# A hybrid decoder step on one core: the Down product's seven results in banks of their own, buffers shared with the gated layer, and higher shares of side work

## The chip, the cores and the metric

The kernel runs on one core of a Trainium2 chip. The core's engines run their own instruction queues side by side: TensorE (PE) for matmuls, with its weight loads as PEld, VectorE (DVE), ScalarE (ACT), GpSimd (POOL) and SyncE (SP), which here issues most transfers. The metric is the device time of one execution in microseconds (us); less is better. TensorE's clock has two levels, 1.2 and 2.4 GHz; the profile gives the granted share of the full one, 1.00 or 0.50, or a mean of both over a stretch.

## The reference

One inference step of a decoder layer, for a prompt of 512 tokens and 8 sample requests of 8 tokens (576 columns T in all), everything in f32:

```
u = rms_norm(x, g_mix) @ w_in                  # 2048 -> conv, SSD and attention inputs
y_a = short_conv_mixer(u_a)                    # gated short convolution
y_b = ssd_mixer(u_b, dt_bias, a_log, d_skip)   # state-space scan: log_a = dt * -exp(a_log)
y_c = nsa_mixer(u_c, paged cache)              # compressed, selected and window attention
x = x + concat(rms_norm(y_a), rms_norm(y_b), rms_norm(y_c)) @ w_out
h = rms_norm(x, g_ffn)
x = x + (silu(h @ w_gate) * (h @ w_up)) @ w_down
```

with dt = softplus(dt_raw + dt_bias). New cache rows and states are outputs too.

## The kernel before

**Products.** Each f32 matrix is split into a high part (`split`: ScalarE rounds it to fp32r, names ending in hi) and a low part (VectorE subtracts, names ending in lo), and a product is three matmuls: hi·hi, lo·hi, hi·lo. All matmuls named below have 288 columns (HALF, half of T). A *plain job* computes 128 rows of a product: weight chunks of 128 x 512 are loaded (raw), split (whi, wlo), multiplied into a PSUM tile pg, and evacuated. An in-projection job has 16 blocks of K x 3 x 2 halves = 96 matmuls.

**The order of the work.** The in-projection runs as jobs1, jobs2 and jobs3 (the last two 12 jobs each). `run_group` steps a pump behind each matmul: `pump.run(369.0 * len(job.halves) * ratio)` issues side work up to an estimated cost of that share of the matmul's time; the ratios in `run_jobs` are the shares. The side work is `chain()`: compress, sample attention (page gathers on GpSimd, scores and sums on TensorE with tiles pt and po, softmax on ScalarE and VectorE), prompt attention, and merge_c, which writes the merged heads into S4. `pump.drain(main)` issues what is left of it. Then x, the residual, is loaded in 24 transfers on SyncE (L1708 to L1710), and the jobs of w_out follow with `ssd()` and merge_a as their side work. `ssd()` first loads dtb (dt_bias) and ea (a_log) on SyncE, applies Exp to ea and to a small tile sd on ScalarE, and computes dt and log_a in small VectorE operations on tiles sd0 to sd6; matmuls with triU, tri64 and ones follow.

The order in which each engine takes its instructions comes from a scheduler that follows the order of the code; where buffers of a pool are all in use, the next user waits for the last reader.

**The gated layer** (gate and up) multiplies block matrices by Strassen's seven products instead of eight: for each of the weights' items, seven operands (called "1" to "7", order "1264375") are formed from four quarters by VectorE, split, and multiplied by X. Their hi and lo parts take turns: three of seven come from the buffers `whi`/`wlo`, four from `fhi`/`flo` of a pool fw. An operand is 12 matmuls.

**Down** (w_down) begins with 16 plain jobs (jobs6[0]) whose inputs ghl are loaded from DRAM (go), split into hi and lo. Then come three ranges r of the inner dimension. A range has 8 *items*, each one pair of output blocks mp with seven products (ORDER "1256473", 12 matmuls each, 84 in all), whose results `evac_d` adds to x1T with VectorE, ScalarE and GpSimd; 16 plain jobs of the range stand partly between the items and partly behind them (`rest`), those behind with `range_ops` of the next range as side work, which forms the seven right operands. `w_ops` forms and splits an item's seven weight operands (f0, f1 for hi and lo). The seven results of an item are in PSUM tiles: three in pt, two in the halves of pa, one in po, one in the first half of pb:

```
pa, pb = pg(), pg()
ps = [pt()[:, :HALF] for _ in range(3)] + [pa[:, 0, :HALF], pa[:, 1, :HALF], po()[:, :HALF], pb[:, 0, :HALF]]
for p, n in zip(ps, ORDER):
```

`g_in` computes the activation of a tile of the next range. Results 16 x 128 columns each leave at the end through tiles ots.

Of the kernel before, what the change touches and what calls it, by code (L numbers as in the profile page):

```python
# [33 lines left out]
KC = 4  # L34
# [42 lines left out]
def hybrid_step_kernel(ctx, tc, x_prompt, x_sample, cache_k, cache_v, cache_win_k, cache_win_v,  # L77
# [76 lines left out]
    def close_pool(guard):  # L154
        guard.__exit__(None, None, None)
# [160 lines left out]

    rstdB = consts.tile([128, T], F32, name="rstdB")

    ssq = consts.tile([128, 5], F32, name="ssq")
# [869 lines left out]
    def ssd():  # L1189
        YB = dp.tile([128, 4, T], F32, name="YB")  # L1190
        sq_b = sq_c
        tiny = lambda name, n=8: dp.tile([128, 5, n], F32, name=name)
        dtb = dp.tile([128, 8], F32, name="dtb")
        nc.sync.dma_start(dtb, dram(dt_bias, 0, [[0, 128], [1, 8]]))
        ea = dp.tile([128, 8], F32, name="ea")
        nc.sync.dma_start(ea, dram(a_log, 0, [[0, 128], [1, 8]]))
        dsk = dp.tile([128, 4], F32, name="dsk")
# [489 lines left out]
    run_jobs(jobs1[2:], 0.8)  # L1687
    run_jobs(jobs2, 0.85)
    run_jobs(jobs3, 1.05)
    pump.drain(main)  # L1690
# [189 lines left out]
    def prep(i):  # L1880
# [16 lines left out]
        for n in "1264375":  # L1897
            if g < NE and n in "12":
                continue
            if n == "6":  # L1900
                s2 = ws(s1, a11, OP.subtract)
            if n == "3":
                s4 = ws(a12, s2, OP.subtract)
            src = {"1": a11, "2": a12, "6": s2, "4": a22, "3": s4, "7": s3, "5": s1}[n]
            p = n_op[0] % 7
            n_op[0] += 1
            pool, pre, bufs = (wpool, "w", 3) if p < 3 else (fw, "f", 4)
            hi = pool.tile([128, KC, 128], F32R, name=pre + "hi", tag=pre + "hi", bufs=bufs)
            lo = pool.tile([128, KC, 128], F32R, name=pre + "lo", tag=pre + "lo", bufs=bufs)
            split(hi, lo, src)  # L1910
            out.append((n, hi, lo))
            tick(600)
            yield
# [71 lines left out]

    close_pool(fwg)
    x1g, x1p = open_pool("x1")
# [14 lines left out]
    def out_rows(m):  # L2002
# [3 lines left out]
        ot = evt(512).rearrange("p (a b) -> p a b", a=4)  # L2006
        ots = fp.tile([128, 128], F32, name="ots", tag="ots", bufs=2)
        ps = pt()
# [54 lines left out]
    def load_d(i):  # L2063
# [3 lines left out]
        loaded[i] = []  # L2067
        for h in range(2):
            for q_ in range(2):
                w = fp.tile([128, KC, 128], F32, name="wr", tag="wr", bufs=8)  # L2070
                nc.sync.dma_start(w, dram(w_down, (12 * r + 4 + 4 * h) * 128 * D + mp * 256 + q_ * 128,
# [3 lines left out]
    def w_ops():  # L2075

        for i in range(len(items)):
            a11, a21, a12, a22 = loaded.pop(i)
            s1 = fp.tile([128, KC, 128], F32, name="ws", tag="ws", bufs=2)
            for n in ORDER:  # L2080
# [6 lines left out]
                src = {"1": a11, "2": a12, "3": a12, "4": a22, "5": s1, "6": a11, "7": a21}[n]  # L2087
                hi, lo = [fp.tile([128, KC, 128], F32R, name=f"f{q_}", tag=f"f{q_}", bufs=4) for q_ in range(2)]
                split(hi, lo, src)
# [58 lines left out]
    for r in range(NR):  # L2148
        rest = list(jobs6[1 + r])
        tiles = list(range(plain[1 + r], plain[1 + r] + 4))  # L2150
        for mp in range(KT // 2):
            if r + 1 == NR and mp == 7:
                tiles = list(range(plain[-1], nf))
            i = r * KT // 2 + mp
            u = evt(HALF)
            pa, pb = pg(), pg()
            ps = [pt()[:, :HALF] for _ in range(3)] + [pa[:, 0, :HALF], pa[:, 1, :HALF], po()[:, :HALF], pb[:, 0, :HALF]]
            for p, n in zip(ps, ORDER):
                next(weights, None)
                hi, lo = made.pop((i, n))  # L2160
# [4 lines left out]
                evac_d(mp, n, p, u)  # L2165
                if tiles and (n in "53" or r + 1 == NR):
                    g_in(tiles.pop(0))

            for _ in range((2, 2, 2, 2, 3, 3, 2, 0)[mp] if r + 1 == NR else mp % 2):
                run_group([rest.pop(0)], 0.0)  # L2170
# [10 lines left out]
    close_pool(fg)  # L2181
    close_pool(x1g)
    close_pool(eg)

# [28 lines left out]
```

## Time and profile before

| | before |
|---|---|
| median of 3 runs | 2990.16 us (2987.16 to 2991.98) |
| profiled execution | 2989.67 us, its span 2987.9 us |
| mean granted clock of TensorE | 0.973 |
| TensorE busy | 2837.6 us (95%) |
| VectorE, ScalarE, GpSimd busy | 73%, 43%, 21% |

The span is what the profile covers; the 1.8 us between it and the execution's time lie around it. Times in the trace count from the start of the span. "Busy" is the sum of an engine's instructions without waits. A wait is told as "engine, tile, line <- what ended it".

### The profile page before, as it was taken

How to read it: one execution, taken by the hardware profiler on the slowest of the kernel's cores; microseconds unless marked ns; L12 is line 12 of the kernel's file. 1: busy time of each engine (PE TensorE's matmuls, PEld its weight loads, DVE VectorE, ACT ScalarE, POOL GpSimd, SP SyncE). 2: the span in 40 equal slices, each digit the busy share in tenths (PEclk: the TensorE clock that was granted, in tenths of full speed). 3: DMA queues.
4: the chain of work that ended last, by engine and by line, in shares of the span. 5: the costliest groups of instructions: out<-in, count | busy, mean ns of one | idle time of the engine just before them, and what ended most of it. 6: DMA issues, size and time to landing. Idle time of an engine off the chain costs nothing.

```text
span 2987.9 us, 57523 instructions
## 1 busy us (share of the span) xinstructions
PE 2837.6 (95%) x22006; PEld 2729.2 (91%) x22006; DVE 2170.7 (73%) x4409; ACT 1283.3 (43%) x2432; POOL 641.2 (21%) x672
## 2 busy tenths in 40 slices
PE   7999998787899998999999999999999999999999
PEld 6999997676789887999999999999999999999998
DVE  5566565444586765757899988888888879889874
ACT  5465563222354553335554444444444434444332
POOL 2342342444343320202001101101101102222120
PEclk9999999898999998999999999999999999999999
DMA  7444333554623214357655433333333354333323
GB/s 234 117 130 124 94 90 84 166 161 144 151 60 79 58 50 138 105 159 215 185 182 172 161 101 108 109 106 108 107 109 109 108 180 125 118 103 118 110 70 111
DMA packets 485660, 370.65 MB, mean 124 GB/s; under 512 B 70121, under 2 KB 444880, under 8 KB 485384
## 3 DMA queue, kind: packets, MB, share of 16 engines
q1 hardware_dynamic: 461656, 306.55, 35.2%
q0 software_dynamic: 20944, 55.13, 6.4%
q10 hardware_dynamic: 2784, 5.29, 0.5%
q8 instruction: 174, 2.85, 0.4%
q14 instruction: 102, 0.84, 0.1%
HBM read 312.98 MB, written 51.79 MB: 122 GB/s over the span
## 4 chain that ended last, share of the span: by engine, by line
PE 49%; DVE 5%; DMA 2%; issue 1%; ACT 1%; SPq 0%; POOL 0%; ACTq 0%; DVEq 0%
PE pg L1949 16%; PE pg L434 12%; PE pt L1949 9%; PE po L1949 5%; PE pg L2164 2%; PE pt L2164 2%; DVE f L96 1%; PE pt L434 1%; PE po L2164 1%; DVE wlo L96 1%; DVE x1T L96 1%; DMA raw<-in_w_up_dram 1%; DMA u<-g_d 1%; DVE wr L96 0%; PE pt L128 0%
## 5 line engine op out<-in xcount | busy, mean ns | idle before, releaser
L93 ACT ACTIVATE whi<-raw 128x512 fp32r<-128x512 f32 (+1 forms) x510 | 319.4, 628 | 536.8 <-PE pg L434 260.7
L96 DVE TENSOR_TENSOR wlo<-raw,whi 128x512 fp32r<-128x512 f32 (+1 forms) x510 | 354.1, 696 | 171.3 <-ACT whi L93 143.3
L434 PE MATMUL pg<-hhi,whi 128*128 128x288 f32 (+1 forms) x1440 | 344.6, 319 | 4.8 <-issue 4.0
L1949 PE MATMUL pg<-X,fhi 128*128 128x288 f32 x1656 | 333.6, 297 | 0.5 <-DVE u L96 0.5
L434 PE MATMUL pg<-hlo,whi 128*128 128x288 f32 (+1 forms) x1440 | 326.0, 306 | 8.1 <-issue 4.7
L434 PE MATMUL pg<-hhi,wlo 128*128 128x288 f32 (+1 forms) x1440 | 324.1, 305 | 7.3 <-issue 4.3
L1949 PEld LDWEIGHTS pg<-X,fhi 128*128 128x128 f32 x1656 | 264.8, 188 | 4.5 <-DVE u L96 0.7
L96 POOL TENSOR_TENSOR u<-u 128x576 f32<-128x576 f32 x44 | 70.9, 1616 | 888.3 <-DVE u L96 811.2
L434 PEld LDWEIGHTS pg<-hhi,whi 128*128 128x128 f32 (+1 forms) x1440 | 238.0, 196 | 20.7 <-issue 17.0
L434 PEld LDWEIGHTS pg<-hlo,whi 128*128 128x128 f32 (+1 forms) x1440 | 241.8, 196 | 13.5 <-issue 8.7
L434 PEld LDWEIGHTS pg<-hhi,wlo 128*128 128x128 f32 (+1 forms) x1440 | 241.5, 196 | 9.6 <-issue 5.9
L93 ACT ACTIVATE fhi<-raw 128x512 fp32r<-128x512 f32 x246 | 155.3, 632 | 212.1 <-PE pg L1949 180.9
L1949 PE MATMUL pg<-X,flo 128*128 128x288 f32 x828 | 239.3, 295 | 0.0
L1949 PE MATMUL pt<-X,whi 128*128 128x288 f32 x1168 | 235.8, 295 | 0.0
L434 PE MATMUL pg<-ghl,whi 128*128 128x288 f32 x1280 | 228.8, 298 | 3.9 <-DVE ghl L96 2.6
L96 DVE TENSOR_TENSOR flo<-raw,fhi 128x512 fp32r<-128x512 f32 x246 | 170.2, 693 | 46.3 <-ACT fhi L93 41.9
L434 PE MATMUL pg<-S,whi 128*128 128x288 f32 x1024 | 197.1, 301 | 0.4 <-DVE u L96 0.4
L434 PEld LDWEIGHTS pg<-ghl,whi 128*128 128x128 f32 x1280 | 190.1, 190 | 4.9 <-DVE ghl L96 2.8
L1949 PEld LDWEIGHTS pt<-X,whi 128*128 128x128 f32 x1168 | 188.2, 188 | 0.0
L96 POOL TENSOR_TENSOR x1T<-x1T,u 128x288 f32<-128x288 f32 (+1 forms) x72 | 99.1, 1376 | 392.7 <-ACT u L93 240.5
L1949 PE MATMUL pt<-X,wlo 128*128 128x288 f32 x584 | 172.9, 296 | 0.0
L434 PEld LDWEIGHTS pg<-S,whi 128*128 128x128 f32 x1024 | 159.0, 191 | 1.4 <-issue 0.6
(1343 smaller groups left out, 6979.0 us busy)
## 6 DMA issues: line engine op xcount, KB each, us to landing
wr<-in_w_gate_dram SPq DMA_DIRECT2D x88, 512.0 KB
wr<-in_w_up_dram SPq DMA_DIRECT2D x88, 512.0 KB
raw<-in_w_in_dram SPq DMA_DIRECT2D x144, 256.0 KB
wr<-in_w_down_dram SPq DMA_DIRECT2D x96, 256.0 KB
raw<-in_w_down_dram SPq DMA_DIRECT2D x80, 256.0 KB
raw<-in_w_out_dram SPq DMA_DIRECT2D x64, 256.0 KB
g_d<-u POOLq DMA_DIRECT2D x44, 288.0 KB
u<-g_d SPq DMA_DIRECT2D x40, 288.0 KB
```

The lines of the kernel that those rows point to most:

```text
L93: S.activation(out, in_, func, bias=bias, scale=scale, accum_out=accum)
L96: (eng or V).tensor_tensor(out, a, b, op=op)
L434: PE.matmul(ps[:m, s, :HALF], w[:, k, :m], x[:, s * HALF:(s + 1) * HALF], start=(k0 + k == 0 and n == 0), stop=(k0 + k == n_k - 1 and n == 2))
L1949: PE.matmul(P[n], w[:, k, :], xx, start=(j == 0 and q_ == 0), stop=(j == 7 and q_ == 2))
L2164: PE.matmul(p, w[:, j, :], x, start=(j == 0 and c_ == 0), stop=(j == 3 and c_ == 2))
```

## The change

It has six parts. (1) ea and dtb are loaded at the start, from GpSimd's queue into a pool that lives for the whole kernel, instead of in `ssd()` from SyncE's. (2) The shares of side work rise from 0.85 to 0.95 in jobs2 and from 1.05 to 1.1 in jobs3. (3) The last gated item's first three operands ("1", "2", "6") use the whi/wlo buffers and the other four fhi/flo; before, the count ran on over all items. (4) The pool fw stays open through Down, and Down's w_down loads (in 5 buffers of 128 x 1024) and operand parts use its buffers instead of ones of Down's own (8 of 128 x 512; f0, f1); ots has one buffer instead of two. (5) Result 4 gets the first half of pb, and result 3 a fourth pt tile; pa holds result 6 alone. (6) In the first two ranges a plain job stands behind six of eight items instead of four (six in the items, ten behind them); in the last range the counts of the 16 jobs are dealt out differently, the tiles of g_in come at products 5 and 3 only, and the last ones start at the seventh item.

```diff
+    ea = consts.tile([128, 8], F32, name="ea")
+    dtb = consts.tile([128, 8], F32, name="dtb")
+    nc.gpsimd.dma_start(ea, dram(a_log, 0, [[0, 128], [1, 8]]))
+    nc.gpsimd.dma_start(dtb, dram(dt_bias, 0, [[0, 128], [1, 8]]))
...
-        dtb = dp.tile([128, 8], F32, name="dtb")
-        nc.sync.dma_start(dtb, dram(dt_bias, 0, [[0, 128], [1, 8]]))
-        ea = dp.tile([128, 8], F32, name="ea")
-        nc.sync.dma_start(ea, dram(a_log, 0, [[0, 128], [1, 8]]))
...
-    run_jobs(jobs2, 0.85)
-    run_jobs(jobs3, 1.05)
+    run_jobs(jobs2, 0.95)
+    run_jobs(jobs3, 1.1)
...
-            p = n_op[0] % 7
+
+            p = n_op[0] % 7 if i + 1 < len(items) else len(out)
...
-    close_pool(fwg)
...
-        ots = fp.tile([128, 128], F32, name="ots", tag="ots", bufs=2)
+        ots = fp.tile([128, 128], F32, name="ots", tag="ots", bufs=1)
...
+            w2 = fw.tile([128, KC, 256], F32, name="wr", tag="wr", bufs=5).rearrange("p a b -> p (a b)")
             for q_ in range(2):
-                w = fp.tile([128, KC, 128], F32, name="wr", tag="wr", bufs=8)
+                w = w2[:, q_ * KC * 128:(q_ + 1) * KC * 128].rearrange("p (k c) -> p k c", k=KC)
...
-                hi, lo = [fp.tile([128, KC, 128], F32R, name=f"f{q_}", tag=f"f{q_}", bufs=4) for q_ in range(2)]
+                hi, lo = [fw.tile([128, KC, 128], F32R, name=q_, tag=q_, bufs=4) for q_ in ("fhi", "flo")]
...
-            if r + 1 == NR and mp == 7:
+            if r + 1 == NR and mp == 6:
...
-            ps = [pt()[:, :HALF] for _ in range(3)] + [pa[:, 0, :HALF], pa[:, 1, :HALF], po()[:, :HALF], pb[:, 0, :HALF]]
+            ps = [pt()[:, :HALF] for _ in range(3)] + [pa[:, 0, :HALF], pb[:, 0, :HALF], po()[:, :HALF], None]
             for p, n in zip(ps, ORDER):
+                p = pt()[:, :HALF] if p is None else p
...
-                if tiles and (n in "53" or r + 1 == NR):
+                if tiles and n in "53":
...
-            for _ in range((2, 2, 2, 2, 3, 3, 2, 0)[mp] if r + 1 == NR else mp % 2):
+            for _ in range((0, 2, 3, 4, 4, 3, 0, 0)[mp] if r + 1 == NR else mp % 4 > 0):
...
     close_pool(x1g)
+    close_pool(fwg)
```

**VectorE at the end of jobs3.** Before, from the last operations of merge_c (S4, qT) to the first of the sd chain; wlo belongs to the weights of w_out here, and x1 is the residual:

```order
L96 TENSOR_TENSOR wlo_13503<-raw_13489,whi_13502 128x512
L105 SCALAR_TENSOR_TENSOR S4_13199<-qT_705,cols_193,S4_13199 128x576 x2
L96 TENSOR_TENSOR wlo_13633<-raw_13492,whi_13632 128x512
L100 TENSOR_SCALAR triU_13569<-diff_110 128x128
L100 TENSOR_SCALAR same_13571<-same_13571,fl8_137 64x64
L96 TENSOR_TENSOR tri64_13574<-same_13571,triU_13569 64x64
L96 TENSOR_TENSOR wlo_13707<-raw_13495,whi_13706 128x512
L96 TENSOR_TENSOR x1_13438<-pg_13485,x1_13438 128x288
L96 TENSOR_TENSOR x1_13446<-pg_13485,x1_13446 128x288
L96 TENSOR_TENSOR x1_13439<-pg_13702,x1_13439 128x288
L96 TENSOR_TENSOR sd0_13534<-dtg_165,dtb_13522 128x40
```
Of the change, the same place on VectorE, from the last S4 operation to the first of the sd chain; wlo belongs to the last chunks of jobs3 here:

```order
L105 SCALAR_TENSOR_TENSOR S4_13014<-qT_709,cols_197,S4_13014 128x576 x2
L96 TENSOR_TENSOR u_13302<-pg_13163,rstdB_189 128x576
L96 TENSOR_TENSOR wlo_13308<-raw_13236,whi_13307 128x512
L96 TENSOR_TENSOR wlo_13336<-raw_13272,whi_13335 128x512
L96 TENSOR_TENSOR u_13302<-u_13302,rstdB_189 128x576
L1412 COPY u_13415<-cols2_198 128x8x2
L96 TENSOR_TENSOR sd0_13534<-dtg_165,dtb_191 128x40
L100 TENSOR_SCALAR triU_13569<-diff_110 128x128
L105 SCALAR_TENSOR_TENSOR sd1_13535<-sd0_13534 128x40
L100 TENSOR_SCALAR sd5_13539<-sd0_13534 128x40
L100 TENSOR_SCALAR same_13571<-same_13571,fl8_137 64x64
L96 TENSOR_TENSOR tri64_13574<-same_13571,triU_13569 64x64
```
The S4 operations now end ahead of jobs3's last splits, and the sd chain begins among these, ahead of the evacuations into x1.

**ScalarE between the gated layer and Down.** Before; whi and raw are weights of Down's first plain jobs, ghl the split of their inputs go:

```order
L93 ACTIVATE u_28703<-pt_28590 128x288
L93 ACTIVATE whi_28826<-raw_28816 128x512
L93 ACTIVATE whi_28874<-raw_28818 128x512
L93 ACTIVATE ghl_28790<-go_28782 128x576
L93 ACTIVATE ghl_28793<-go_28783 128x576
L93 ACTIVATE ghl_28796<-go_28784 128x576
L93 ACTIVATE ghl_28799<-go_28785 128x576
L93 ACTIVATE whi_28915<-raw_28820 128x512
```
Of the change; fhi are the first weight operands of Down's items, made from wr and ws:

```order
L93 ACTIVATE u_28703<-pt_28590 128x288
L93 ACTIVATE whi_28825<-raw_28815 128x512
L93 ACTIVATE whi_28873<-raw_28817 128x512
L93 ACTIVATE fhi_29478<-wr_28996 128x512
L93 ACTIVATE fhi_29482<-wr_28999 128x512
L93 ACTIVATE fhi_29495<-ws_29477 128x512
L93 ACTIVATE ghl_28789<-go_28781 128x576
L93 ACTIVATE ghl_28792<-go_28782 128x576
L93 ACTIVATE ghl_28795<-go_28783 128x576
L93 ACTIVATE ghl_28798<-go_28784 128x576
L93 ACTIVATE whi_28914<-raw_28819 128x512
```
Three fhi have moved ahead of the ghl splits, and the whi in front use buffers of other operands of the last gated item.

**TensorE in the first item of Down.** Before, from the end of result 6 (first half of pg_29492) through result 7 (po) into result 4 (second half of the same pg):

```order
L2164 MATMUL pg_29492<-go_29372,f1_29521 128x288
L2164 MATMUL po_29497<-go_28949,f0_29559 128x288 x2
L2164 MATMUL po_29497<-go_28949,f1_29560 128x288
L2164 MATMUL po_29497<-go_29127,f0_29559 128x288 x2
L2164 MATMUL po_29497<-go_29127,f1_29560 128x288
L2164 MATMUL po_29497<-go_29256,f0_29559 128x288 x2
L2164 MATMUL pg_29492<-go_28945,f0_29537 128x288 x2
L2164 MATMUL pg_29492<-go_28945,f1_29538 128x288
```
Of the change, from the end of result 6 through result 4 (pg_29488) to the start of result 7 (po):

```order
L2166 MATMUL pg_29487<-go_29367,flo_29516 128x288
L2166 MATMUL pg_29488<-go_28944,fhi_29532 128x288 x2
L2166 MATMUL pg_29488<-go_28944,flo_29533 128x288
L2166 MATMUL pg_29488<-go_29079,fhi_29532 128x288 x2
L2166 MATMUL pg_29488<-go_29079,flo_29533 128x288
L2166 MATMUL pg_29488<-go_29247,fhi_29532 128x288 x2
L2166 MATMUL pg_29488<-go_29247,flo_29533 128x288
L2166 MATMUL pg_29488<-go_29371,fhi_29532 128x288 x2
L2166 MATMUL pg_29488<-go_29371,flo_29533 128x288
L2166 MATMUL po_29492<-go_28948,fhi_29554 128x288 x2
```
Result 4 has a pg tile of its own and follows result 6 at once; before, it shares result 6's tile and begins when most of result 7 has been issued.

## Rows read from the trace of the kernel before

**Rows 1.** The page: busy time by engine; granted clock of TensorE in 40 slices.

```profile
PE 2837.6 (95%) x22006; PEld 2729.2 (91%) x22006; DVE 2170.7 (73%) x4409; ACT 1283.3 (43%) x2432; POOL 641.2 (21%) x672
...
PEclk9999999898999998999999999999999999999999
```

**Rows 2.** Windows before and in Down: length, busy (instructions) by engine, PEclk, DMA share, GB/s.

```profile
2400.00:2420.00 20.00, 20.00 (x152) 20.00 (x152) 13.22 (x23) 9.21 (x16) 0.00 (x0) 1.00 0.23 66
2580.00:2600.00 20.00, 18.23 (x126) 18.00 (x125) 17.19 (x31) 6.90 (x13) 3.16 (x3) 0.91 0.43 138
```

**Rows 3.** Windows of the seams and of sample attention, same columns.

```profile
1149.90:1190.10 40.20, 27.60 (x155) 25.30 (x153) 22.62 (x71) 6.87 (x17) 5.22 (x6) 0.75 0.70 202
1190.10:1193.60 3.50, 3.50 (x16) 3.44 (x16) 2.06 (x7) 1.05 (x3) 0.00 (x0) 0.50 0.47 149
500.00:800.00 300.00, 236.55 (x2258) 196.21 (x2254) 130.17 (x372) 69.06 (x127) 125.28 (x132) 0.86 0.50 150
2426.17:2436.00 9.83, 6.10 (x26) 5.87 (x27) 6.44 (x7) 2.83 (x5) 4.28 (x4) 0.66 0.88 290
```

**Rows 4.** Waits of TensorE, 2380 to 2990 us: total, times, longest.

```profile
PE pg L2164 <- DVE u L96: 8.4, 9, 1.8
```

**Rows 5.** Waits of TensorE, 1149 to 1194 us.

```profile
PE pt L120 <- DVE sd L105: 6.6, 1, 6.6
PE pg L434 <- DVE wlo L96: 4.9, 1, 4.9
```

**Rows 6.** Timeline of SyncE, 1149 to 1170 us: start, duration, issue.

```profile
1149.85 0.37 SPq L1708 DMA_DIRECT2D x<-xT_d  x1
...
1164.80 0.53 SPq L1710 DMA_DIRECT2D x<-xS_d  x1
...
1166.89 0.37 SPq L1196 DMA_DIRECT2D ea<-in_a_log_dram  x1
```

**Rows 7.** Waits of ScalarE, 1149 to 1194 us.

```profile
ACT ea L93 <- DMA ea<-in_a_log_dram: 6.9, 1, 6.9
```

**Rows 8.** Timeline of VectorE, 1160 to 1180 us: sd, first and last.

```profile
1172.35 0.19 DVE L96 TENSOR_TENSOR sd<-dtg,dtb 128x40 f32<-128x40 f32 x1
...
1178.54 0.42 DVE L1228 COPY lab<-sd 64x512 f32<-64x512 f32 x1
```

**Rows 9.** Waits of TensorE, 490 to 800 us.

```profile
PE po L120 <- issue: 14.8, 27, 1.8
PE po L120 <- ACT pT L93: 13.3, 4, 6.3
...
PE pt L120 <- ACT kT L93: 5.2, 4, 1.8
```

**Rows 10.** Waits of GpSimd, 490 to 800 us.

```profile
POOL vp L271 <- PE po L120: 84.9, 10, 12.7
```

**Rows 11.** Waits of TensorE, 2424 to 2437 us.

```profile
PE pg L434 <- DVE ghl L96: 2.6, 1, 2.6
PE pg L434 <- ACT ghl L93: 1.2, 1, 1.2
```

**Rows 12.** Waits of ScalarE, 2415 to 2437 us.

```profile
ACT whi L93 <- PE po L1949: 8.5, 2, 7.5
```

**Rows 13.** Timeline of TensorE, 2503.5 to 2506 us: idle time and releaser in brackets.

```profile
2505.43 0.79 PE L2164 MATMUL pg<-go,f 128*128 128x288 f32 x4 [1.25 <-DVE u L96]
```

**Rows 14.** Groups of VectorE, 2490 to 2740 us: busy, mean ns, idle before.

```profile
L96 DVE TENSOR_TENSOR f<-wr,f 128x512 fp32r<-128x512 f32 x94 | 66.2, 706 | 1.9 <-ACT f L93 1.4
...
L96 DVE TENSOR_TENSOR f<-ws,f 128x512 fp32r<-128x512 f32 x16 | 28.3, 1768 | 0.0
```

**Rows 15.** Tile rows: durations in ns (least, median, most), first and last start.

```profile
L348 POOL DMA_DIRECT2D rows<-in_norm_ffn_dram x1: 682/682/682, 2.5 to 2.5; - x1
```

**Rows 16.** Tile ots, same columns.

```profile
L2014 DVE COPY ots<-pt x16: 294/295/298, 2926.6 to 2983.2; 64x128 f32<-64x128 f32 x16
L2016 SPq DMA_DIRECT2D out_dram<-ots x16: 467/472/524, 2927.6 to 2983.5; - x16
```

## The prediction

> **What bounds the kernel now.** I read the page's busy times and its row of granted clock first: TensorE works 95% of the span, and the other engines have room [rows 1]. A change that leaves TensorE's instructions as they are (the two programs have 20,733 each) can save only the time in which TensorE stands, or runs at the lower of its two clock levels. So I looked for that time stretch by stretch. At full clock 152 matmuls fill 20.00 us, 0.1316 us each [rows 2]; a stretch's count times 0.1316 is what it needs, and the rest is lost. Four places stand out that the diff touches: the seam between the in-projection and the output projection (155 matmuls in 40.20 us), the 500 to 800 us of sample attention (TensorE busy 236.55 of 300 at 0.86 of the clock), the seam between the gated layer and Down (26 in 9.83) [rows 3], and nine stalls inside Down's items [rows 4]. Everything else of TensorE runs dense and can only be moved.
>
> **A, the first seam (ea and dtb loaded early, shares raised).** The 155 matmuls need 155 × 0.1316 = 20.4 us and take 40.2: 19.8 lost; the next 3.5 us hold 16 at half clock (0.50), 16 × 0.1316 = 2.1, so 1.4 more [rows 3]: 21.2 in all. The chain of waits shows two stops, 4.9 us for a wlo (VectorE, which first finishes the merge of attention's heads, S4) and 6.6 us for sd [rows 5]; half clock behind them is the rest. Behind the second stop stands a queue. pump.drain ends attention; then SP issues 24 loads of x, from 1149.85 to 1165.33, and only then ea, at 1166.89 [rows 6]. ScalarE waits 6.9 us for ea [rows 7], with sd's exponential queued behind it, and VectorE's 25 small sd operations run from 1172.35 to 1178.54 [rows 8] with nothing else to do. TensorE takes its instructions in order, and the matmuls on sd stand ahead of the next projection job.
>
> After: ea and dtb are there from the start, and the higher shares bring the end of attention forward by about a job and a half. The order shows the S4 operations some ten rows ahead of jobs3's last chunks on VectorE, and the sd chain between the last splits of jobs3 and the first of jobs4. Both stops thus have projection work in front of them. I leave one stop of the size of the first, 4.9 less rounding: **−21.2 + 4.2 = −17**. Bounds: −8 (only the ea wait and a part of the half clock behind it go, because the 24 loads of x, which now stand behind five weight loads on SP, hold up the first evacuations) and −21 (all).
>
> **B, what the shares cost.** run_group lets the pump put so much side work behind each matmul; counted in the two orders, sample attention is spread over 8.24 projection jobs' matmuls before and 7.26 after, prompt attention over 11.76 and 11.24. That takes 1.50 jobs × 96 matmuls × 0.1316 = 19 us of cover out of stages in which TensorE already stands 63.45 of 300 us [rows 3]. These matmuls aren't lost, they run later, dense. So the cost is what the stages don't shrink. Of the stops there, 18.5 us wait for ScalarE's pT and kT, a result just asked for; the largest other one, 14.8, waits for nothing the profile shows [rows 9]. GpSimd's page gathers wait 84.9 us for TensorE [rows 10], so most of the chain runs behind TensorE, and less cover makes it run sooner. I let a fifth of the cover return as stops: **+4**. Bounds: 0, and +19 if the stages are as long as their own chains.
>
> **C, the second seam (operands of the last gated item, shared buffers).** 26 matmuls need 3.4 us of the 9.83: 6.4 lost [rows 3]. TensorE waits 2.6 and 1.2 for ghl [rows 11], the split of Down's first inputs; their hi halves stand on ScalarE behind a whi that waited 7.5 us, to the last matmul of the last gated item (po) [rows 12], because that buffer was held by its op "5". Now op "6" of that item holds it, four operations earlier. But the order puts three fhi of w_down ahead of ghl, and the third needs the buffer of op "7", the last but one; an op is 12 matmuls, 1.6 us. The ghl splits thus start about 1.6 us before the item's end instead of after it, and four of them and their lo halves follow. I leave 1.4 us: **−5**. Bounds −1 (the fhi take the place of whi: the wait is for op "7" and the sum of two w_down loads) and −6.4.
>
> **D, Down's items.** VectorE's read of the first half of pa (result 6) and TensorE's writing of the second half (result 4) can't overlap: TensorE stops until that read ends, 9 times, 8.4 us, the longest 1.8 [rows 4]; in one of them it resumes at 2505.43 [rows 13]. All other results have a bank each. The clock stays at 1.00 around the 1.25 us stop, but falls to 0.91 where the longest lies (126 matmuls in 20 us: 16.6 needed, 3.4 lost, 1.8 of it the stop), so 1.6 more [rows 2]. Giving 4 a pg tile and 3 a pt tile removes the cause: 10.0. Against it: two more plain jobs per range leave the run of plain jobs behind the items, so its VectorE work on the next range's operands is divided over 10 jobs instead of 12; a plain job is 24 matmuls, 3.2 us. VectorE is the second busiest, its f<-ws take 1.768 us against 0.706 of f<-wr [rows 14]. I allow 1: **−9**. Bounds −12 (VectorE's backlog in the pairs goes too) and −4 (half of the stops come back as waits for lo splits).
>
> Those long f<-ws run while GpSimd adds to x1T. The Trainium skill ("SBUF — State Buffer", section "Who interferes with whom") states that a VectorE operation with two inputs in SBUF and a GpSimd one exclude each other on a shared read port. By that rule, denser items would meet more such blocks: 16 × 1.06 us in two ranges is what this pattern costs VectorE now, and TensorE only where VectorE is behind. The trace agrees as to the durations.
>
> **E, F, at nothing.** The two early loads cost GpSimd an issue each, like the 0.68 us of the rows load that follows them [rows 15]; ScalarE's first split waits for a weight load until then anyway; 0, at worst +1.4. The single ots buffer: 16 copies from 2926.6 to 2983.2, 3.8 us apart, with an issue of 0.47 us each [rows 16], which leaves 3 us for the store; 0, at worst +1. The last range's table only deals the same 16 plain jobs out differently.
>
> **Sum.** −17 + 4 − 5 − 9 = −27, against the profiled execution: 2989.67 − 27 = 2962.7, **2963 us**. That execution lies 0.5 below the median of 2990.16, so the same sum fits either. All good ends: −21 + 0 − 6.4 − 12 = −39.4, 2950. All bad: −8 + 19 − 1 − 4 + 2.4 = +8.4, 2998. A measurement of this kernel can tell about 0.2%, 6 us, from no change.
>
> **Rivals.**
> Fixed wall (15%): sample and prompt attention keep their length, because each step waits for its own ScalarE and VectorE results; B is +19 and the sum −12: 2978. For it: pT's four stops, up to 6.3 us. Against: the gathers that wait for TensorE.
> VectorE bounds Down (13%): the bank wait goes, but TensorE then waits for lo splits at the next weight load; D is −2 and the sum −20: 2970. For it: VectorE's share in Down; against: items between two plain jobs, in the last range, show no stop but one.
> The seam stays (10%): S4 or the x loads take the place of the sd chain; A is −8, the sum −18: 2972. The bank split not reaching the program is no case, since the order shows 4 and 7 in tiles of their own.
> Slower (7%): with less cover, TensorE's granted clock falls in sample attention. Its stops there already cost 0.14 of the clock [rows 3]. The work is 236.55 × 0.86 = 203 full-speed us; at 0.86 it fills 236.55, at 0.74 it takes 275, 38 more: −27 + 38 = +11, 3001. It decides from a mean clock of 0.75 down (271 us, +34, +7). Against: the clock is full where projection is interleaved, and nine tenths of that stay.
> The Trainium skill ("TensorE: Matmul & The Clock Gate", section "What's actually happening") has the gate follow how busy TensorE has recently been, and thinner cover is what would lower it; the trace agrees in direction, half clock after the two stops of [rows 5], full after 1.25 us ones.
>
> **How the numbers follow.** My forecast has 55% (own range 2955 to 2969); with it the first three rivals make 93%, at 2955 to 2982. The range takes in the good end and a fixed wall with one more small term short: **2950 to 2985**. Slower by over 0.2% is the clock's case and part of a mix of bad ends, 6%; within 0.2% the milder part of both, 9%; faster 85%.
>
> **What would show it.** Right: no wait for ea, and none over 3 us for sd or wlo at the first seam; its window at 25 us instead of 40; no wait of Down's matmuls for u<-pg; under 2 us for ghl. B shows in TensorE's idle time and clock in sample attention, which should be within 5 us of 63. Wrong: a clock there well under 0.86, or new waits of Down's matmuls for f or of its plain jobs for wlo, which would put the gain of D back.

## The result, and the profile after

The changed kernel takes 2962.16 us in the median of 4 runs (2956.48 to 2970.22), the kernel before in the same session 2989.69 (4 runs): a ratio of 0.991, 95% interval 0.9884 to 0.9936. That is 27.5 us less; 2963 was forecast. Run again in another session, it took 2952.8 against 2976.92, 0.9923 (0.991 to 0.9936). The four times spread over 14 us, and the profiled execution is the slowest of them: 2970.22, its span 2968.4, 19.5 below that of before. Sums over its trace are held against those 19.5.

The page of the changed kernel, as in [rows 1]:

```profile
PE 2834.8 (96%) x22006; PEld 2726.6 (92%) x22006; DVE 2169.8 (73%) x4409; ACT 1282.8 (43%) x2432; POOL 643.7 (22%) x674
...
PEclk9999899788999999999999999999999999999999
```
TensorE's matmuls are as many as before and its busy time is nearly what it was; the 19.5 us come out of its idle time, and the dip of its clock around the first seam, in the sixteenth slice, is gone. That of sample attention, the eighth to tenth slice, is still there and reads 7, 8, 8 instead of 8, 9, 8.

Windows of the changed kernel, as in [rows 3]: sample attention, the first 19.98 us behind the last in-projection matmul, and the first 9.83 us behind the gated layer's last:

```profile
500.00:800.00 300.00, 236.39 (x2226) 193.52 (x2224) 128.51 (x367) 68.78 (x126) 131.56 (x135) 0.85 0.48 148
1166.66:1186.64 19.98, 19.98 (x158) 19.23 (x157) 11.99 (x39) 6.39 (x14) 3.64 (x3) 1.00 1.06 289
2426.37:2436.20 9.83, 9.29 (x68) 9.07 (x68) 9.83 (x15) 4.74 (x8) 4.44 (x4) 1.00 0.91 292
```
The first seam holds 158 matmuls in 19.98 us, at full clock and without a gap, where 155 took 40.20 [rows 3]. The second holds 68 instead of 26. In sample attention TensorE stands 63.6 of 300 us, as before, at 0.85 instead of 0.86. But this fixed window now holds 2226 matmuls instead of 2258 [rows 3], so it doesn't show what the stage costs as a whole. The whole of jobs2 and jobs3, before and changed, does:

```profile
477.48:1150.08 672.60, 599.16 (x5265) 526.27 (x5264) 394.13 (x1247) 249.25 (x589) 250.72 (x277) 0.93 0.39 105
```
```profile
482.79:1166.66 683.87, 607.77 (x5265) 533.12 (x5264) 409.87 (x1283) 250.35 (x592) 253.51 (x280) 0.92 0.39 105
```
The same 5265 matmuls take 11.3 us longer. TensorE stands 76.1 us instead of 73.4, which is 2.7 of them; the other 8.6 are busy time, at a lower mean clock.

TensorE's waits from 1149 to 1210 us answer to [rows 5]; all that is left over a microsecond is this:

```profile
PE pg L438 <- DVE wlo L96: 1.3, 1, 1.3
```
From 490 to 800 us they answer to [rows 9]:

```profile
PE po L120 <- issue: 23.7, 40, 1.1
PE pt L120 <- issue: 11.5, 8, 2.8
...
PE po L120 <- ACT pT L93: 0.8, 2, 0.7
```
The long stops for pT have nearly gone, and the ones that wait for nothing shown have grown from 14.8 us in 27 to 23.7 in 40. From 2370 to 2990 us, the whole of Down, they answer to [rows 4] and [rows 11], and these four are all there is:

```profile
PE pt L128 <- issue: 1.0, 1, 1.0
PE pt L2166 <- DVE x1T L96: 0.4, 2, 0.3
PE pg L438 <- DVE u L96: 0.4, 1, 0.4
PE pg L438 <- DVE x1T L96: 0.2, 1, 0.2
```
No stop for u<-pg at result 4 is left of 8.4 us, and none for ghl. ScalarE's timeline at the second seam (start, duration, wait in brackets) shows the order that the prediction was worked from:

```profile
2422.14 0.63 ACT L93 ACTIVATE fhi<-wr 128x512 fp32r<-128x512 f32 x1 [1.77 <-PE pg L1950]
2423.07 0.63 ACT L93 ACTIVATE fhi<-wr 128x512 fp32r<-128x512 f32 x1 [0.30 <-PE pg L1950]
2424.68 0.64 ACT L93 ACTIVATE fhi<-ws 128x512 fp32r<-128x512 f32 x1 [0.97 <-PE pg L1950]
2425.22 0.67 ACT L93 ACTIVATE ghl<-go 128x576 fp32r<-128x576 f32 x1
2426.61 2.17 ACT L93 ACTIVATE ghl<-go 128x576 fp32r<-128x576 f32 x3 [0.73 <-DMA go<-g_d]
```
Three fhi wait for the last gated item's operations, and ghl begins 1.15 us before the gated layer ends at 2426.37; before, it began 0.44 us behind its end, at 2426.61 against 2426.17:

```profile
2426.61 2.39 ACT L93 ACTIVATE ghl<-go 128x576 fp32r<-128x576 f32 x4
```

For the experiments the span is cut at the same instructions in every trace (start of the first projection matmul, end of jobs1 and so on); each cell is one profiled execution. The output projection here runs from the end of jobs3 to its own last matmul; "to items" from the gated layer's end to the first item's first matmul.

| kernel | session | start | jobs1 | jobs2, 3 | output proj. | gated | to items | items |
|---|---|---|---|---|---|---|---|---|
| before | 1 | 15.85 | 461.63 | 672.60 | 280.05 | 953.86 | 58.85 | 436.61 |
| changed | 1 | 18.18 | 464.61 | 683.87 | 259.91 | 955.91 | 52.85 | 423.43 |
| banks alone | 2 | 16.87 | 456.58 | 666.32 | 280.27 | 953.05 | 58.85 | 433.09 |
| table alone | 2 | 16.50 | 457.10 | 666.22 | 280.29 | 954.36 | 58.73 | 432.60 |
| shares alone | 2 | 16.59 | 461.07 | 679.58 | 261.60 | 953.31 | 57.35 | 436.57 |
| early loads alone | 2 | 17.70 | 454.37 | 663.44 | 278.51 | 956.52 | 57.72 | 438.05 |
| changed, again | 3 | 18.03 | 459.12 | 670.04 | 260.82 | 955.28 | 52.70 | 423.31 |
| changed, old item rule | 3 | 17.93 | 456.96 | 682.05 | 260.69 | 956.12 | 56.50 | 422.57 |
| changed, old shares | 3 | 17.41 | 460.70 | 662.11 | 278.54 | 956.04 | 52.98 | 422.82 |
| changed, shares 0.85, 1.15 | 3 | 18.27 | 458.81 | 660.28 | 273.09 | 956.56 | 53.14 | 423.13 |
| changed, own buffers | 4 | 18.12 | 449.33 | 576.64 | 259.99 | 955.27 | 56.55 | 424.40 |
| banks and table | 4 | 16.80 | 446.10 | 573.05 | 280.30 | 954.67 | 58.08 | 423.59 |
| item rule alone | 4 | 16.81 | 445.93 | 569.16 | 277.64 | 953.55 | 57.03 | 437.86 |
| changed, late loads | 4 | 16.58 | 451.07 | 579.71 | 261.58 | 954.08 | 53.49 | 422.95 |

The kernels of a session ran on one chip; sessions 2 to 4 on three different ones. From the output projection on, equal code takes equal time within 1 to 3 us: the output projection takes 277.64 to 280.30 in the five kernels without the higher shares and the early loads, and "to items" 57.35 to 58.85 in the six kernels with the old item rule and the old buffers. jobs1 to jobs3 vary by 5 to 14 us from execution to execution, and jobs2 and jobs3 are another stage altogether in session 4 (below).

### The profile page after: what moved, and what is told of

Its sections match the earlier page's. It is cut to its first block, busy times and chain, and to the rows that moved or that the text cites. A ratio compares the mean times of both kernels' runs of the same rounds, so it can differ in the third digit from the quotient of the medians.

```text
span 2968.4 us, 57509 instructions
## 1 busy us (share of the span) xinstructions
PE 2834.8 (96%) x22006; PEld 2726.6 (92%) x22006; DVE 2169.8 (73%) x4409; ACT 1282.8 (43%) x2432; POOL 643.7 (22%) x674
## 4 chain that ended last, share of the span: by engine, by line
PE 49%; DVE 5%; DMA 2%; issue 1%; ACT 1%; POOL 0%; SPq 0%; ACTq 0%; DVEq 0%; POOLq 0%
PE pg L1950 16%; PE pg L438 10%; PE pt L1950 9%; PE po L1950 5%; PE pt L2166 4%; PE pg L2166 2%; DVE wlo L96 1%; PE po L2166 1%; PE pt L438 1%; DMA raw<-in_w_up_dram 1%; DVE go L96 1%; DVE u L96 1%; DVE x1T L96 1%; DVE flo L96 1%; PE pt L128 0%
## 5 line engine op out<-in xcount | busy, mean ns | idle before, releaser
L93 ACT ACTIVATE fhi<-wr 128x512 fp32r<-128x512 f32 x222 | 140.0, 631 | 219.2 <-PE pg L1950 89.0
L96 DVE TENSOR_TENSOR flo<-wr,fhi 128x512 fp32r<-128x512 f32 x222 | 160.3, 722 | 49.6 <-ACT fhi L93 48.5
```

Of the source, the lines that this page charges most:

```text
L93: S.activation(out, in_, func, bias=bias, scale=scale, accum_out=accum)
L96: (eng or V).tensor_tensor(out, a, b, op=op)
```

## The experiments

**Down: banks alone.** The kernel before with

```diff
-ps = [...3 pt...] + [pa[:, 0, :HALF], pa[:, 1, :HALF], po()[:, :HALF], pb[:, 0, :HALF]]
+ps = [...3 pt...] + [pa[:, 0, :HALF], pb[:, 0, :HALF], po()[:, :HALF], None]    # None: pt()
```

> The kernel before with the bank split of Down's results alone (result 4 in a pg tile of its own, result 3 in a fourth pt tile). Bank theory: the nine stops of 8.4 us in Down's items go, and the lowered clock behind the longest with them: 8 to 11 us faster, about 2980. Rival, VectorE bounds the items: the stops come back as waits for the lo parts of operands, and the gain is 0 to 4 us.

Measured: 2972.01 us against 2979.29, ratio 0.9976 (0.9962 to 0.9989). The 7.3 us lie between the theory's 8 to 11 and the rival's 0 to 4. The stops for u are gone, but the items, all that the edit touches, are only 3.5 us shorter. TensorE's waits in Down of this kernel:

```profile
PE pt L2165 <- DVE x1T L96: 4.9, 4, 2.7
PE pg L434 <- DVE x1T L96: 3.9, 2, 2.0
```
8.8 us in 6 stops for x1T have come in place of 8.4 us in 9 for u. VectorE's timeline ahead of one of them, which ends at 2515.78:

```profile
2499.14 0.68 DVE L96 TENSOR_TENSOR f<-ws,f 128x512 fp32r<-128x512 f32 x1
2499.73 1.92 DVE L96 TENSOR_TENSOR wr<-wr 128x512 f32<-128x512 f32 x1
2501.57 0.44 DVE L96 TENSOR_TENSOR x1T<-pt,x1T 128x288 f32<-128x288 f32 x1
```
VectorE runs from 2496.30 to 2512 us with no gap over 0.1 us, its wr<-wr stretched to 1.92 us, and its reads of finished results (x1T<-pt) come late; TensorE meets the next use of their banks. The VectorE rival holds, with x1T in place of f.

**Down: the table alone.** The kernel before with `mp % 4 > 0` and the last range's new counts and tiles.

> The kernel before with the new table of plain jobs alone (six of eight items followed by one in the first two ranges, the other deal in the last), the results' banks as before. Bank theory: the stops stay where two items follow each other, two pairs a range in the first two instead of four, and the last range has two pairs as well; 2 to 5 us faster. Rival, the plain jobs are what removes the stops, since VectorE catches up behind them: 8 to 11 us faster. If the table costs by VectorE's work divided over fewer jobs, it shows in the run of plain jobs behind the items: up to 4 us slower.

Measured: 2972.8 us, ratio 0.9982 (0.9969 to 0.9996): 6.5 us less, between the two forecasts; items 4.0 us shorter. The waits for u, as in [rows 4]:

```profile
PE pg L2164 <- DVE u L96: 5.0, 6, 1.2
```
Four of the nine stops go, those of the pairs that a plain job now parts, and one comes in the last range, between its first two items, which the new table leaves together. The stops are where the bank theory had them. The run of plain jobs behind the items doesn't get longer by it.

**Down: both.** The kernel before with the two edits above together.

> The kernel before with the bank split and the new table of plain jobs together, nothing else. Alone they shortened the items from 436.6 to 433.1 and 432.6 us, 3.5 and 4.0. Theory (the banks take the stop away, the plain jobs give VectorE the time without which it becomes the next stop): together 422 to 425 us, more than the sum, and 12 to 14 us faster than before, about 0.9955. Rival (they add up, and the shared buffers made the rest of the change's 423.4): 428 to 430 us.

Measured: 2856.3 us against 2872.9, ratio 0.9946 (0.9934 to 0.9958), items 423.59, 13.0 us shorter. The time, 16.6 us less, is beyond the expected 12 to 14, the items are as expected. Alone the edits give 3.5 and 4.0. TensorE's waits in Down over 0.3 us (beside the one at the end):

```profile
PE pg L434 <- DVE ghl L96: 2.6, 1, 2.6
PE pg L434 <- ACT ghl L93: 1.2, 1, 1.2
...
PE pt L2165 <- ACT f L93: 0.7, 1, 0.7
PE pg L2165 <- DVE f L96: 0.5, 1, 0.5
```
Neither u nor x1T is left; the two of ghl belong to the second seam. The theory of the pair holds: the banks remove the stop, and the plain jobs give VectorE the time without which it makes the next one.

**The first seam: shares alone.** The kernel before with 0.95 and 1.1.

> The kernel before with the higher shares of side work alone; ea and dtb are still loaded behind the 24 loads of x. Theory: sample attention costs 4 to 11 us more, and the first stop of the seam (4.9 us for wlo) goes with the half clock behind it, 6 to 10 us; the second (for ea and the sd chain) stays in part. Net -5 to +4 us. Rival, the shares alone bring the whole gain of the seam, 20 us, since the ea load too comes earlier: net -8 to -16.

Measured: 2970.56 us against 2979.29, ratio 0.9972 (0.9959 to 0.9985). Output projection 18.7 us shorter than in the two kernels above it on the same chip (280.3), jobs2 and jobs3 13.3 longer (666.3). The waits of TensorE from 1110 to 1200 us, as in [rows 5]:

```profile
PE pt L120 <- DVE mt L96: 1.5, 1, 1.5
PE pg L434 <- DVE wlo L96: 1.1, 2, 0.6
PE pt L120 <- DVE sq_c L96: 1.0, 1, 1.0
```
Both stops are gone, 6.6 and 4.9 us. The load of ea, still issued in `ssd()`, comes early as well, as the rival had it: SyncE issues it ahead of the 24 loads of x, 12.2 us before jobs3 ends at 1157.24.

```profile
1145.02 0.42 SPq L1196 DMA_DIRECT2D ea<-in_a_log_dram  x1
...
1159.09 0.56 SPq L1708 DMA_DIRECT2D x<-xT_d  x1
```
So the end of attention and the load of ea move together here, and this run doesn't tell which of them counts. The net of 8.7 us lies in the rival's range; the cost of 13.3 is above the theory's 4 to 11. Here too it is mostly busy time: jobs2 and jobs3 of the table alone, and of the shares alone:

```profile
473.60:1139.82 666.22, 597.13 (x5265) 527.66 (x5264) 394.05 (x1247) 248.85 (x589) 250.74 (x277) 0.93 0.38 106
```
```profile
477.66:1157.24 679.58, 607.25 (x5265) 533.88 (x5264) 410.35 (x1284) 250.92 (x594) 250.20 (x280) 0.92 0.38 105
```
TensorE stands 69.1 and 72.3 us in them, so stops are 3.2 of the 13.4 us between these two.

**The first seam: early loads alone.** The kernel before with ea and dtb loaded at the start.

> The kernel before with the early loads of ea and dtb alone. Theory: ScalarE's wait of 6.9 us for ea goes and the second stop of the seam (6.6 us) shrinks to what the sd chain itself takes, with a part of the half clock: 5 to 10 us faster; the start is not later by more than 1.4 us. Rival from the trace of the change, where the first projection matmul stands 2.3 us later and the end of the first 21 jobs 5.3 us later: the two loads delay the start, and the net is only 0 to 5 us.

Measured: 2979.92 us against 2979.29, ratio 0.9999 (0.9987 to 1.0012): nothing, the low end of the rival. The same waits:

```profile
PE pg L438 <- DVE wlo L96: 4.9, 1, 4.9
PE pg L438 <- ACT whi L93: 2.8, 1, 2.8
PE pt L128 <- DMA xc<-XB_d: 2.5, 1, 2.5
...
PE pt L120 <- DVE sd L105: 0.6, 1, 0.6
```
The stop for sd has shrunk from 6.6 to 0.6 us, so the late ea was a cause of it. But stops for xc (2.5) and whi (2.8) have come in its place, and that for wlo stands: the last S4 operation begins 9.8 us behind the end of jobs3, as before, where in the change it begins 13.7 us ahead of it. The output projection is 1.8 us shorter than in the neighbours, no more than equal code varies. Against that the first projection matmul stands 1.1 us later than in the neighbours and the gated layer takes 2 to 3.5 us more.

**Old shares in the changed kernel.** 0.85 and 1.05, everything else as changed.

> The changed kernel with the old shares 0.85 and 1.05. With the shares alone the time from the end of the in-projection to the end of the output projection fell from 280.3 to 261.6 us and that of jobs2 and jobs3 rose from 666.3 to 679.6. So here: the former 278 to 280, the latter 663 to 667, and the time 4 to 7 us above the change. Rival (the early loads of ea and dtb are what counts in the seam): the former is under 270 and the time is that of the change or less.

Measured: 2960.24 us, ratio 0.9943 (0.993 to 0.9956); the changed kernel beside it 2952.8, 0.9923. Output projection 278.54, jobs2 and jobs3 662.11: the theory's numbers within a microsecond, and the time 7.4 us above the change, just over the 4 to 7 expected. In jobs2 and jobs3 TensorE stands 68.8 us here and 70.0 in the changed kernel beside it; the rest of the 7.9 us between the two is busy time.

**The changed kernel again,** beside the last:

> The changed kernel once more, beside the kernels that undo one part of it, since its four times lay between 2956 and 2970. It should be 0.9 to 1.1% faster than the kernel before on the same chip. Theory on the start: the first projection matmul, 2.3 us later in the first profile than in the kernel before, is within a microsecond of the others here, as the stage varies by itself; rival: it is at 18 us again, as in the kernel with the early loads alone (17.7), and the two loads cost 1 to 2 us.

Measured: 2952.8 us (2950.01 to 2957.53), 0.77% faster than the kernel before, short of the 0.9 to 1.1 expected. Its jobs2 and jobs3 took 670.04 us, 13.8 less than in the first trace of the same program: so much that stage varies. The start is at 18.03 again; the rival holds.

**Other shares.** The changed kernel with 0.85 in jobs2 and 1.15 in jobs3.

> The changed kernel with the share of jobs2 at the old 0.85 and that of jobs3 at 1.15, which by the order brings the last S4 operation to the same place on VectorE as in the change. Theory (the cost of the shares lies in sample attention, which jobs2 covers): jobs2 and jobs3 take 4 to 10 us less than in the change, the output projection as in the change, 260 to 262, and the time is 3 to 9 us less. Rival (the cost is only side work that moved from behind the end of jobs3 to ahead of it): the sum of both stretches is that of the change, within 2 us.

Measured, in the same session: 2951.93 us, ratio 0.9912 (0.9895 to 0.9928), against 0.9923 of the change: no difference that the intervals allow. jobs2 and jobs3 take 660.28, but the output projection 273.09, where the theory had 260 to 262: stops of 3.3 us for whi and 1.5 for sd are left, and the sd chain begins 5.2 us ahead of the end of jobs3, in the change 10.1. The sum of both stretches is 933.4 us against 930.9, 2.5 apart where the rival allowed 2. Since equal code in jobs2 and jobs3 differs by up to 12 us between two kernels of session 3, the sum decides nothing; the theory's short projection is refuted.

**The second seam: old item rule.** The changed kernel with `p = n_op[0] % 7` for all items.

> The changed kernel with the old rule for the last gated item's buffers (count modulo 7). Theory: ScalarE's whi again waits for the last operation of that item with ghl queued behind it, and the stretch from the end of the gated layer to the first item, 52.85 us in the change against 58.85 before, is 57 to 59 again; 4 to 6 us slower than the change. Rival: it is the shared buffers, by which w_down is loaded and split early, that shortened the stretch; then it stays below 55.

Measured: 2963.1 us, ratio 0.9949 (0.9936 to 0.9961). All five runs lie above all five of the changed kernel beside it, by 10.3 us in the medians, but the traces put 12.0 us in jobs2 and jobs3, where the code is the same, and only 3.8 in the stretch; what made the former longer stays open. The stretch is 56.50 us, between the theories, with no stop for ghl. Its first 9.83 us read as in the change, so the shared buffers alone clear the seam itself:

```profile
2416.61:2426.44 9.83, 9.26 (x68) 9.05 (x68) 9.83 (x15) 4.26 (x8) 4.42 (x4) 1.00 0.85 271
```
What lengthens the stretch comes 23 us into it, a stop of 2.2 us that ends at 2439.53; behind it the mean clock to the end of the stretch is 0.95. In the waits of Down it is this:

```profile
PE pg L438 <- DVE x1T L96: 2.4, 2, 2.2
```
Whether the old rule makes that stop isn't shown.

**The second seam: own buffers.** The changed kernel with Down's buffers as before:

```diff
+    close_pool(fwg)
     x1g, x1p = open_pool("x1")
-            w2 = fw.tile([128, KC, 256], F32, name="wr", tag="wr", bufs=5)...
+                w = fp.tile([128, KC, 128], F32, name="wr", tag="wr", bufs=8)
-                hi, lo = [fw.tile(..., tag=q_, bufs=4) for q_ in ("fhi", "flo")]
+                hi, lo = [fp.tile(..., tag=f"f{q_}", bufs=4) for q_ in range(2)]
```

> The changed kernel with Down's weights and operand parts in buffers of their own again (and two ots buffers), the pool fw closed before Down as in the kernel before; the new rule for the last gated item stays. Rule theory: the stretch from the gated layer's end to the first item stays at 52 to 54 us. Buffer theory (the order with the old rule and shared buffers lost nothing to ghl): TensorE waits for ghl again, and the stretch is 55 to 59. The items should take 422 to 425 us whichever holds, if banks and table alone carry them; 427 or more if the shared buffers had a part in that.

Measured: 2850.76 us against 2872.9, ratio 0.9922 (0.9909 to 0.9935). The stretch is 56.55 us: the buffer theory's; items 424.40, which the buffers have little part in. The rule alone frees ScalarE of the wait behind whi, but the first ghl then waits for the load of go, and VectorE's timeline behind the gated layer's end, at 2301.30, shows what comes between. ScalarE, then VectorE:

```profile
2300.76 0.68 ACT L93 ACTIVATE ghl<-go 128x576 fp32r<-128x576 f32 x1 [5.46 <-DMA go<-g_d]
```
```profile
2302.08 1.88 DVE L96 TENSOR_TENSOR ghl<-go,ghl 128x576 fp32r<-128x576 f32 x1
2303.88 1.68 DVE L96 TENSOR_TENSOR go<-u,go 128x288 fp32r<-128x288 f32 x1
2305.48 2.08 DVE L96 TENSOR_TENSOR ghl<-go,ghl 128x576 fp32r<-128x576 f32 x3
```
A split of go, of a later operand, stands between the first and the other three lo halves of ghl. Here the fourth ends 6.3 us behind the gated layer's end; in the change it ends 3.7 us behind it, at 2430.04:

```profile
2429.29 0.75 DVE L96 TENSOR_TENSOR ghl<-go,ghl 128x576 fp32r<-128x576 f32 x1
```

**The second seam: the rule alone.** The kernel before with the new rule.

> The kernel before with the new rule for the last gated item's buffers alone. Rule theory, as the prediction had it: whi no longer waits for the last operation, ghl is split earlier, and the stretch of 58.85 us falls to 53 to 55. Buffer theory: it stays at 57 to 59, as go is loaded no earlier. Time: 0 to 5 us faster.

Measured: 2869.22 us, ratio 0.9992 (0.9984 to 1.0001); the stretch is 57.03, at the low edge of the buffer theory, and 0.3 below the shortest of the six kernels with neither part (57.35 to 58.85, mean 58.26). The five kernels with both take 52.70 to 53.49, mean 53.03. So both together are worth 5.2 us by the means; either part alone, 56.50 to 57.03 in three kernels, is worth 1 to 2, little more than equal code varies.

**Late loads: a candidate.** The changed kernel with ea and dtb loaded in `ssd()` as before.

> The changed kernel without the early loads of ea and dtb, which are issued in ssd again: a candidate. In the kernels with the early loads the first projection matmul stands at 17.4 to 18.3 us, without them at 15.9 to 16.9, and the gated layer takes 955.3 to 956.6 against 953.1 to 954.4; the output projection with the shares alone was as short as in the change. Theory: 2 to 4 us faster than the change, a ratio of about 0.991. Rival (the early loads are needed for the seam): the output projection is 4 us or more above 261, and the time is that of the change or more.

Measured: 2845.88 us against 2872.9, ratio 0.9903 (0.9888 to 0.9917), the lowest ratio of all. Output projection 261.58, first matmul at 16.58, gated layer 954.08: the theory's numbers. The change itself wasn't among the kernels of session 4; its ratios elsewhere, 0.991 and 0.9923, have intervals that overlap this one, so whether the candidate beats it is not settled. The load of ea is issued 12.2 us ahead of the end of jobs3 here, as with the shares alone; the early loads aren't needed for the seam.

## Why the prediction came out right, and which of its steps did not

The time was met within 1 us, partly since misses cancel, and partly by luck of the executions: the sum was formed on the profiled execution, and between the two profiled ones the difference is 19.5 us, not 27; in another session the medians are 24.1 apart.

**A, predicted −17.** The seam's window went from 40.20 us for 155 matmuls to 19.98 for 158, the output projection from 280.05 to 259.91: −20.1, near the good end. The bound of lost time was well read from count times 0.1316. The sum left in one stop of 4.9 us (with the whole of it the term would be −16.3); 1.3 us of it is there. The wait for ea was real, but the early loads aren't what ended it: they alone bring 1.8 us of the output projection, the shares alone 18.7, and these bring the load of ea ahead of the end of jobs3 too. With ea early and attention late, other stops take the place of the one for sd. What the kernels with a short output projection have in common is that attention ends, and the sd chain starts, while jobs3 still runs.

**B, predicted +4.** This is the term that was mis-sized. The same two windows hold the same number of matmuls before and after (5265 in jobs2 and jobs3, 2067 in the output projection), so no TensorE work moved across their border. The stage grew by 11.3 us between the first two traces, 13.3 for the shares alone and 7.9 in session 3. (One execution of this stage says little by itself; the four traces of sessions 1 to 3 with 0.95 in jobs2 have a mean of 678.9 us, the six with 0.85 one of 665.2.) The +4 for cover that returns as stops was enough: TensorE stands 72.4 us in the mean of the four and 70.6 in that of the six. What the sum put at nothing is the clock: TensorE is busy 606.5 us in the four and 594.6 in the six with the same matmuls, at mean clocks of 0.92 to 0.93 and 0.93 to 0.95. That is the slower rival's mechanism in a milder form. The rival's +38 and its clock of 0.75 didn't come, and the sign that the prediction named, a window of fixed length, reads 0.85 for 0.86 since it holds less of the work. The clock also differs between executions with equal shares, 0.92 and 0.93 for 682.05 and 670.04 us, so it isn't set by the shares alone. The fixed wall's +19 overshot, and its reason doesn't show: the stops for pT fell from 13.3 to 0.8 us.

A and B together were to give −13; by the times the shares give −8.7 us (2979.29 to 2970.56) and −7.4 (2960.24 to 2952.8).

**C, predicted −5.** −6.0, 58.85 to 52.85 us. Three fhi ahead of ghl, waiting for the last item's operations, the ghl splits before the layer's end: the trace shows these steps as written. But the reason given, that op "6" holds the buffer in place of op "5", isn't what ended the stop for ghl. With the old rule and the shared buffers the seam is clear as well, and 3.65 us are lost later; with the rule alone ghl waits for the load of go, and VectorE puts a split of go among its lo halves. What the prediction didn't see is that only the two parts together gave the whole in these runs.

**D, predicted −9, bound −12.** −13.2, 436.61 to 423.43. The stops (8.4) and the clock behind the longest (1.6) are the 10.0 of the prediction. Beyond them an item without any stop takes 11.29 us before (first to next matmul, in the last range) and 11.15 in the change, 11.11 with the banks alone, while the table alone leaves it at 11.29: 24 × 0.14 = 3.4 us that no listed wait shows. 10.0 + 3.4 = 13.4. These 3.4 are the same wait, too short to be listed. In 13 of the 15 items of before without a stop, the first matmul of result 4 starts 0.06 us after VectorE's read of result 6 ends, and it and the next one are spaced 0.18 to 0.22 and 0.24 us from the one in front instead of 0.13. With a bank for each result no such step is there. One of the 13, VectorE and then TensorE:

```profile
2820.55 0.46 DVE L96 TENSOR_TENSOR u<-pg,u 128x288 f32<-128x288 f32 x1 [0.23 <-PE pg L2164]
```
```profile
2821.06 1.85 PE L2164 MATMUL pg<-go,f 128*128 128x288 f32 x12
```
So the term fell short by items that looked free of stops. The point that VectorE would take back a part is true of the banks alone, 8.8 us; the table that was costed at 1 us is what prevents it.

**E, predicted 0, at worst +1.4.** The first projection matmul stands at 17.41 to 18.27 us in the seven kernels with early loads and at 15.85 to 16.87 in the seven without: means 17.95 and 16.57, +1.4, the worst case of the term. ScalarE's first split does wait for a weight load, but that split starts at 13.77 instead of 12.80 us in the mean, and the Exp of ea now stands between it and the first matmul, where the way takes about 0.25 us more. Why the load lands later wasn't tried. And the gated layer takes 955.27 to 956.56 in the former, 953.05 to 954.67 in the latter, means 955.96 and 953.84: +2.1, which the prediction didn't have at all. **F, predicted 0:** from the last item to the last matmul 61.56 before and 61.37 after.

Together, with A and B at −8, C −6, D −13.2, E +3.5: −23.7, against measured −27.5 and −24.1 (2976.92 to 2952.8). In the first two traces the stages give −20.1 and +11.3 for A and B, −6.0, −13.2, +4.4 for E, and +4.1 in stages that no term covers, most of it jobs1 (+3.0): −19.5.

## What to carry to other kernels

Where one engine is at 95%, cut its trace at the same instructions, count what each stretch needs at full rate, and read the rest: that sized the seams and the stops within a few microseconds before anything ran. Removing a wait for a bank pays only if the engine that empties the banks has time, so look at what that engine does in the stretch before counting the whole wait; here two edits of 3.5 and 4.0 us gave 13.0 together. And when side work is issued faster to clear a later seam, price the clock of the stage that loses cover as well as its stops: here the stops grew by 2 us and the busy time of the same matmuls by 12.

## What the runs showed of the hardware that was not expected

**Another chip, another stage.** On the chip of session 4 the kernel before took 2872.9 us (17 runs) instead of 2977 to 2990, with jobs2 and jobs3 at 569 to 580 us instead of 660 to 684, jobs1 at 446 to 451 instead of 454 to 465, and all stages behind them as elsewhere. The window of sample attention before on the first chip, and of the candidate in session 4:

```profile
490.00:800.00 310.00, 246.47 (x2333) 205.12 (x2333) 138.47 (x400) 71.69 (x132) 131.58 (x140) 0.86 0.49 147
```
```profile
490.00:700.00 210.00, 206.94 (x2385) 181.26 (x2380) 135.35 (x387) 76.87 (x141) 140.71 (x148) 1.00 0.79 232
```
TensorE stands 3 of 210 us instead of 64 of 310 and keeps its full clock, and the transfers run at 232 GB/s instead of 147. Its waits there in the candidate are two:

```profile
PE pt L128 <- DMA kp<-in_cache_k_dram,idxS: 2.6, 1, 2.6
PE po L120 <- ACT pT L93: 0.2, 1, 0.2
```
None of the stops without a shown cause ("issue") is left in that window. The bytes moved are the same (370.6 MB). The program is the same, so something outside of it lengthens sample attention in the first three sessions; what it is, and whether it belongs to the chip or to the session, stays open. The price of the shares changes with it: 577 and 580 us with the higher ones, 573 and 569 with the old, +7 instead of +13.

**The gated layer's rate.** With the early loads, 1000 of its matmuls take 133.93 to 134.14 us in the middle of the layer, without them 133.78 to 133.86 (no stops in either). Nothing in the layer's code differs; two small tiles more in the pool at the start are the one edit that all slower kernels share. The cause wasn't tried.
